# Summing the weights of a small product on VectorE instead of in the DMA, and moving stores from GpSimd's queue to ScalarE's, in a two-layer encoder trunk

## The chip, the cores and the metric

The kernel runs on one core of one Trainium2 chip. TensorE (PE in the profile) multiplies, and its weight loads are shown apart (PEld); VectorE (DVE), ScalarE (ACT) and GpSimd (POOL) work beside it, and 16 DMA engines move data. DMAs are issued by SP, by ACT or by POOL. The metric is the device time of one execution in microseconds (us); lower is better.

## The reference

The input is one sequence of 512 tokens of width 2048, all in float32. Layer 1 is gated grouped-query attention (16 heads, 4 groups of keys and values), layer 2 a gated bidirectional retention with 8 heads. After each layer comes a residual and a layer norm:

```python
proj = h @ w_in                       # layer 2: w_in is 2048 x 12288
q, k, v, g = split(proj)              # 8 heads: 256 + 256 + 512 + 512 columns a head
q, k = rope(q), rope(k) * dk ** -0.5
o = sum over both directions of (q k^T * decay) v
y = (head_group_norm(o) * silu(g)) @ w_out
x = layer_norm(ALPHA * x + y)
```

Nearly all of the arithmetic is in the projections, that is in products of a 512 x 2048 matrix with weight matrices.

## The kernel before, in words

**Products.** Each projection is computed in blocks of 1024 weight columns as two by two quarters by a scheme of the Strassen kind: seven products in place of eight, numbered 1 to 7, each of one sum of feature quarters with one sum of weight quarters. The feature sums ("forms") are made once, the weight sums are made while the weights stream in. The unit of work is a *chunk*, a 128 x 1024 piece of one product's weights in float32. ScalarE rounds it to a high part (`whi`), VectorE subtracts that from the chunk for a low part (`wlo`), both at line 122, and TensorE does three matmuls for each pair of pieces (lines 307 to 309). A chunk of a block is 12 matmuls.

**Small products.** In layer 2's input projection eight of the twelve blocks form four pairs (`PAIRED`). The two product 2s of a pair are put together and split once more into seven small products, the blocks `r_inside`; a chunk of one of them is 6 matmuls and each has two chunks. Their weights are pieces of the two blocks of the pair. A small block knows its first block as `twin`; no other block has one. The table `WITHIN` says after which chunk of the pair each chunk of a small product stands. Small product 5 needs the sum of two pieces, one from each block of the pair (quarters 11 and 12 of the small block).

**How a weight sum is made.** Some sums are made in the DMA: `onto` issues from POOL a DMA that adds its data to a tile that is already loaded. Others are made by a VectorE addition in `make`. In the kernel before, the sum of small product 5 is of the first kind: a hook at product 7 of the pair's second block calls `fetch_sum`, which loads quarter 11 by SP and then lets POOL add quarter 12. The sums of small product 3 and of the large product 6 are additions on VectorE.

**Order.** The list `order` holds all chunks in the order in which TensorE uses them. `next_chunk` keeps two chunks ready ahead of use (`AHEAD`) and, before it makes one, has fetched those up to three further on (`FETCH`). TensorE's instructions stand in the order in which the program is written. Those of the other engines are ordered by a scheduler when the program is built, with buffers as they become free in its own reckoning; at run time each engine takes its own list strictly in order, and an instruction that waits holds up all behind it. Raw pieces go to a pool of nine buffers of 128 x 1024, high and low parts to pools of three each.

**Stores.** The results of the input projection go to device memory and come back head by head: values (`vD2`), gates after SiLU (`gD2`, shown as gDr) and the rotated and transposed queries and keys (`qkD`). All of these stores are issued by POOL in the kernel before. POOL's queue also carries the adding DMAs (line 153) and the stores of the scaled residual (`yD2`). Queries and keys are copied out of TensorE's transposes by ScalarE (line 1196) right before their store, and gates come out of ScalarE's SiLU (line 1189).

**The residual.** Hooks load the first layer's output piece by piece (`load_residual`, line 1154), VectorE scales it (lines 1161 and 1162) and POOL stores it.

Of the kernel before, what the change touches and what calls it, by code (L numbers as in the profile page):

```python
# [33 lines left out]
FETCH = 3  # L34
# [15 lines left out]
PAIRED = ((2, 3), (4, 5), (6, 7), (8, 9))  # L50
# [8 lines left out]
def encoder_trunk_kernel(  # L59
# [19 lines left out]
    nc = tc.nc  # L79
# [13 lines left out]
    def nm(s):  # L93
        n_names[0] += 1
        return f"{s}{n_names[0]}"
# [4 lines left out]
    def x4(name, dt=F32R):  # L100
        return xp.tile([P, 1024], dt, tag="x", name=nm(name))

    def temp(name):
        return tmp.tile([P, 512], F32, tag="temp", name=nm(name))
# [4 lines left out]
    def in_dram(name, shape):  # L109
        return dram.tile(shape, F32, name=name)  # L110

    def v4(x):
        return x.rearrange("p (n d) -> p n d", d=P)
# [4 lines left out]
    def tcols(t):  # L118
        return slice(t * P, t * P + P)
# [10 lines left out]
    order = []  # L130

    def raw_load(src, large=False):
        raw = x4("raw", F32) if large else rp.tile([P, CH], F32, tag="raw", name=nm("raw"))
        x = nc.sync.dma_start(out=raw, in_=src)
        if fetched[0] < 12:
            in_turn(x)
        return raw

    def in_turn(x):

        tc.keep_in_program_order(x)
# [5 lines left out]
    def behind(x, y):  # L147

        tc.add_manual_dep(x.ins, y.ins.name, mybir.DependencyInfo(
            mybir.DependencyClass.NoSync, mybir.DependencyReason.DATA), reason="behind")  # L150
# [4 lines left out]
    class Block:  # L155
# [20 lines left out]
        def fetch(self, p, c):  # L176
            q = lambda n: self.quarter(n, c)
            g = self.got
            if p in (1, 2) and self.twin:
                at = 2, c + 2 * (p == 2)  # L180
                if at not in self.twin.got:
                    self.twin.got[at] = raw_load(q(11 if p == 1 else 21))
                g[p, c] = self.twin.got[at]
            elif p == 1:
                g[1 if self.first else "v", c] = raw_load(q(11), self.hold)
            elif p == 2:
                g[2, c] = raw_load(q(21))
            elif p == (3 if self.idle else 6):
                g[3, c] = raw_load(q(22), self.wide)
            elif p == 4 and self.again and not self.lean and (not self.shared or (2, c) not in g):  # L190
                g[2, c] = raw_load(q(21))
            elif p == 5 and self.first:
                if self.hold:
                    g["v", c] = g[1, c]
                else:
                    self.fetch_sum(c)
# [6 lines left out]
        def make(self, p, c):  # L203

            g, v = self.got, self.got.get(("v", c))
            if p == (3 if self.rows == 1 else 6) and (self.rows == 1 or not self.idle):
                nc.vector.tensor_add(v, v, g[3, c])  # L207
            elif p == 4 and not self.lean:
                x = nc.vector.tensor_add(v, v, g[2, c])  # L209
                if self.nc == 4:  # L210
                    behind(x, los[-3])
            if p in (3, 7):
                return g[3, c]
            return g[p, c] if p == 2 or p == 1 and self.first else v
# [53 lines left out]
    ready = []  # L268
    fetched, taken = [0], [0]

    def fetch_to(n):
        while fetched[0] < min(len(order), n):
            blk, p, c = order[fetched[0]]
            blk.fetch(p, c)
            fetched[0] += 1

    def make_chunk():
        blk, p, c = order[len(ready)]
        raw = blk.make(p, c)
        if p >= blk.keep if isinstance(blk, Plain) else p in blk.kept:  # L280
            hi, lo = x4("wkh"), x4("wkl")
        else:
            hi, lo = [wp.tile([P, CH], F32R, tag=n, name=nm(n)) for n in ("whi", "wlo")]
        los.append(split(hi, lo, raw, len(ready) < 7))
        his.append(casts[-1])
        blk.follow(p, c)
        if p == 1 and blk is a_in[1]:
            a_in[0].add_held(c, hi)
        if p == 7 and blk in r_in and blk.lean and blk.again and c in (0, 2):
            blk.add_behind(hi, blk.got["v", 2 + c // 2], 21, 2 + c // 2)  # L290
        ready.append([(half(hi, j), half(lo, j)) for j in range(2)])

    def next_chunk():

        i = taken[0]
        taken[0] += 1
        while len(ready) < min(len(order), i + 1 + AHEAD):
            fetch_to(len(ready) + 1 + FETCH)
            make_chunk()
        r = ready[i]  # L300
        ready[i] = None
        return r
# [125 lines left out]
    def turn_soon(gen, t, src, own):  # L428

        if not own:  # L430
            o = temp("c")
            nc.scalar.copy(o, src)
            src = o
        steps.append(gen(t, src))
# [29 lines left out]
    def hook(blk, p, c, fn, *args):  # L464
        blk.hooks.setdefault((p, c), []).append(lambda: fn(*args))
# [117 lines left out]
    def transpose4(src, b=None):  # L583
        b = b or bank("tr")
        for i in range(4):
            nc.tensor.transpose(out=b[:, tcols(i)], in_=src[:, tcols(i)], identity=ident)  # L586
        return b
# [3 lines left out]
    r_in = [Block(a["wr_in"][g], g < 2, again=g == 0 or any(g in p for p in PAIRED), lean=any(g == p[1] for p in PAIRED))  # L591
            for g in range(R_G)]
# [5 lines left out]
    r_inside = [Block(Quarters(a["wr_in"][i], a["wr_in"][j]), True, 2, idle=True, rows=1, twin=r_in[i])  # L598
                for i, j in PAIRED]
# [85 lines left out]
    def out_half(total, po, pl, op):  # L685


        def chunk(blk, *at):
            ks = next_chunk()
            for h in blk.hooks.get(at, ()):  # L690
                h()
            run_later()
            return ks
# [417 lines left out]
    qkD, vD2, gD2 = [[in_dram(f"{n}{h}", [P, 4, 512]) for h in range(R_HEADS)] for n in ("qkD", "vDr", "gDr")]  # L1111
# [59 lines left out]
    def rope_2(t, src, put):  # L1171

        m1, m2 = temp("m1"), temp("m2")
        xv, av, bv = [m.rearrange("p (i j r c) -> p i j r c", i=2, j=2, r=2) for m in (src, m1, m2)]
        cb, sb = [m[:, t].unsqueeze(1).broadcast_to([P, 2, 2, 64]) for m in (cos2, sin2)]
        for r in range(2):
            nc.vector.tensor_tensor(out=av[:, :, :, r], in0=xv[:, :, :, r], in1=cb, op=ALU.mult)
            nc.vector.tensor_tensor(out=bv[:, :, :, r], in0=xv[:, :, :, 1 - r], in1=sb, op=ALU.mult)
            yield
        for r in range(2):  # L1180
            nc.vector.tensor_tensor(out=av[:, :, :, r], in0=av[:, :, :, r], in1=bv[:, :, :, r],
                                    op=ALU.subtract if r == 0 else ALU.add)
        soon(3, put, m1)

    def deliver_2(blk, nb, t, src, own):
        pr, kind = divmod(r_in.index(blk), 3)
        if kind == 2:
            o = src if own else temp("gt")
            nc.scalar.activation(o, src, AF.Silu)
            nc.gpsimd.dma_start(out=gD2[2 * pr + nb][:, t], in_=o)  # L1190
        elif nb == 1:
            nc.gpsimd.dma_start(out=vD2[2 * pr + kind][:, t], in_=src)
        else:
            def put(m):
                o = temp("qkT")
                nc.scalar.copy(o, transpose4(m))  # L1196
                stored.add((2 * pr + kind, t))
                nc.gpsimd.dma_start(out=qkD[2 * pr + kind][:, :, tcols(t)], in_=v4(o))  # L1198

            turn_soon(lambda t, src: rope_2(t, src, put), t, src, own)  # L1200

# [154 lines left out]


    ev2, inside = spill(deliver_2), Inside(x2)
    hook(r_in[2], 6, 0, lambda: steps.append(inside.forms()))
    for n, (_, b) in enumerate(PAIRED):  # L1360
        for c in range(2):
            hook(r_in[b], 7, c, r_inside[n].fetch_sum, c)
    paused.append(True)
    for i in range(2):
        hook(r_in[0], 1, 2 * i, x2.form, 2, i)
    work = Stream(out_full(total, a_last, op_a[1]), in_stream(r_in, x2, ev2, (inside, put_together(deliver_2))))
    for r in range(2):
        for t in (2 * r, 2 * r + 1):
# [120 lines left out]
```

## Time and profile before

| What | Value |
|---|---|
| Median of 3 runs | 2089.72 us |
| Lowest and highest run | 2084.93 and 2091.35 us |
| Profiled execution, its time and its span | 2091.57 us, 2089.8 us |
| Mean granted TensorE clock in it | 0.997 |
| TensorE busy | 2066.4 us (99%) |
| VectorE, ScalarE, GpSimd busy | 1645.2, 1192.9, 478.2 us |
| DMA | 420.17 MB, mean 201 GB/s |

A row of the profile gives the source line, the engine, the operation, what it writes and reads by the program's names, and times in us; "idle before" is how long the engine had stood idle, and the arrow names what ended that. The busy time of TensorE is modelled from pipelined matmuls, so that a stall shows as idle time of some tenths of a microsecond less than the stretch between the starts of two matmuls.

### The profile page before, as it was taken

How to read it: one execution, taken by the hardware profiler on the slowest of the kernel's cores; microseconds unless marked ns; L12 is line 12 of the kernel's file. 1: busy time of each engine (PE TensorE's matmuls, PEld its weight loads, DVE VectorE, ACT ScalarE, POOL GpSimd, SP SyncE). 2: the span in 40 equal slices, each digit the busy share in tenths (PEclk: the TensorE clock that was granted, in tenths of full speed). 3: DMA queues.
4: the chain of work that ended last, by engine and by line, in shares of the span. 5: the costliest groups of instructions: out<-in, count | busy, mean ns of one | idle time of the engine just before them, and what ended most of it. 6: DMA issues, size and time to landing. Idle time of an engine off the chain costs nothing.

```text
span 2089.8 us, 26695 instructions
## 1 busy us (share of the span) xinstructions
PE 2066.4 (99%) x9586; PEld 1710.3 (82%) x9586; DVE 1645.2 (79%) x2224; ACT 1192.9 (57%) x1586; POOL 478.2 (23%) x579
## 2 busy tenths in 40 slices
PE   9999999999999999999999999999999999999997
PEld 7888888888888888888887788888788888888886
DVE  7788877889678887776785786876786887979786
ACT  6556546667656754554554454554456665656554
POOL 1145212122222113112213112213211122212112
PEclk9999999999999999999999999999999999999999
DMA  9777958457599879479779779879785677777875
GB/s 345 191 176 214 302 146 197 131 166 159 132 253 229 264 173 231 111 205 221 184 216 240 194 213 224 212 208 233 198 254 161 187 184 191 180 191 183 210 218 114
DMA packets 129749, 420.17 MB, mean 201 GB/s; under 512 B 15696, under 2 KB 18768, under 8 KB 129360
## 3 DMA queue, kind: packets, MB, share of 16 engines
q0 software_dynamic: 60256, 196.11, 45.8%
q1 hardware_dynamic: 68784, 221.30, 30.3%
q8 instruction: 75, 1.23, 0.2%
q10 hardware_dynamic: 576, 1.05, 0.1%
q14 instruction: 58, 0.48, 0.1%
HBM read 349.20 MB, written 71.30 MB: 201 GB/s over the span
## 4 chain that ended last, share of the span: by engine, by line
PE 86%; DMA 7%; issue 3%; DVE 2%; POOL 1%; ACT 1%; SPq 0%; POOLq 0%; ACTq 0%; DVEq 0%
PE acc L308 24%; PE acc L309 24%; PE acc L307 24%; DMA raw<-in_wr_in_dram 4%; PE tr L586 3%; PE o L307 2%; PE o L309 2%; PE o L308 2%; DMA raw<-in_wa_in_dram 1%; PE s L307 1%; PE s L309 1%; PE s L308 1%; DVE wlo L122 1%; DMA xf<-in_xq_dram 1%; ACT whi L122 1%
## 5 line engine op out<-in xcount | busy, mean ns | idle before, releaser
L122 DVE TENSOR_TENSOR wlo<-raw,whi 128x1024 fp32r<-128x1024 f32 (+1 forms) x658 | 798.9, 1219 | 317.7 <-ACT whi L122 315.0
L122 ACT CAST whi<-raw 128x1024 fp32r<-128x1024 f32 (+1 forms) x658 | 687.2, 1050 | 627.0 <-PE acc L309 456.0
L307 PE MATMUL acc<-whi,f 128*128 128x512 f32 x2464 | 972.5, 395 | 4.3 <-DVE t L646 2.4
L308 PE MATMUL acc<-wlo,f 128*128 128x512 f32 x2464 | 962.8, 391 | 5.8 <-DVE wlo L122 5.8
L309 PE MATMUL acc<-whi,f 128*128 128x512 f32 x2464 | 962.0, 390 | 0.0
L308 PEld LDWEIGHTS acc<-wlo,f 128*128 128x128 f32 x2464 | 464.1, 188 | 103.3 <-DVE wlo L122 11.8
L307 PEld LDWEIGHTS acc<-whi,f 128*128 128x128 f32 x2464 | 463.8, 188 | 97.8 <-issue 3.3
L309 PEld LDWEIGHTS acc<-whi,f 128*128 128x128 f32 x2464 | 463.4, 188 | 97.9
L153 POOL DMA_DIRECT2D raw<-in_wr_in_dram x140 | 123.4, 886 | 411.2 <-DVE wlo L122 338.2
L207 DVE TENSOR_TENSOR raw<-raw,raw 128x1024 f32<-128x1024 f32 x94 | 114.7, 1226 | 12.1 <-DMA raw<-in_wr_in_dram 8.8
L476 ACT COPY t<-acc 128x512 f32<-128x512 f32 x150 | 85.0, 587 | 44.4 <-PE acc L309 40.2
L122 DVE TENSOR_TENSOR f<-xf,f 128x1024 fp32r<-128x1024 f32 (+2 forms) x74 | 86.5, 1175 | 7.4 <-ACT f L122 7.4
L122 ACT CAST f<-xf 128x1024 fp32r<-128x1024 f32 (+2 forms) x74 | 74.7, 1015 | 20.1 <-DVE xf L362 5.5
L153 POOL DMA_DIRECT2D raw<-in_wa_in_dram x48 | 42.2, 879 | 154.8 <-DVE wlo L122 113.7
L153 POOL DMA_DIRECT2D yD<-t x48 | 43.8, 1018 | 119.9 <-DVE t L488 37.2
L569 POOL TENSOR_TENSOR rstd<-rs_e,neg_half 128x1 f32<-128x1 f32 x40 | 31.9, 797 | 171.1 <-DVE rs_e L568 170.0
L209 DVE TENSOR_TENSOR raw<-raw,raw 128x1024 f32<-128x1024 f32 x52 | 63.1, 1217 | 0.2 <-DMA raw<-in_wr_in_dram 0.2
L1198 POOL DMA_DIRECT2D qkD<-qkT x32 | 24.3, 759 | 154.4 <-ACT qkT L1196 153.8
L997 ACT ACTIVATE p<-s,nmax 128x512 f32<-128x512 f32 x64 | 44.1, 688 | 20.0 <-DVE s L995 15.1
L1279 ACT ACTIVATE o<-o,nmr,rstd 128x512 f32<-128x512 f32 x32 | 24.9, 778 | 52.4 <-DVE nmr L580 52.2
L995 DVE TENSOR_SCALAR_CACHE_REDUCE s<-s,q_rs 128x512 f32<-128x512 f32 x64 | 48.0, 752 | 7.2 <-PE s L309 6.8
L307 PE MATMUL o<-inh,pTh 128*128 128x512 f32 x128 | 51.4, 402 | 0.0
(210 smaller groups left out, 2191.6 us busy)
## 6 DMA issues: line engine op xcount, KB each, us to landing
raw<-in_wr_in_dram SPq DMA_DIRECT2D x156, 512.0 KB, 5.4
raw<-in_wr_in_dram POOLq DMA_DIRECT2D x140, 512.0 KB, 7.2
raw<-in_wa_in_dram SPq DMA_DIRECT2D x66, 512.0 KB, 6.6
raw<-in_wa_in_dram POOLq DMA_DIRECT2D x48, 512.0 KB, 7.4
raw<-in_wr_p_dram SPq DMA_DIRECT2D x36, 512.0 KB, 4.9
yD<-t POOLq DMA_DIRECT2D x48, 256.0 KB, 6.4
raw<-in_wr_p_dram POOLq DMA_DIRECT2D x24, 512.0 KB, 7.6
y<-yD SPq DMA_DIRECT2D x16, 512.0 KB, 7.2
```

What stands on the lines that cost most here:

```text
L122: x, y = nc.scalar.copy(hi, src), nc.vector.tensor_sub(lo, src, hi.bitcast(F32))
L153: return nc.gpsimd.dma_start(out=x, in_=src, accum_op=ALU.add)
L207: nc.vector.tensor_add(v, v, g[3, c])
L209: x = nc.vector.tensor_add(v, v, g[2, c])
L307: nc.tensor.matmul(ps, sh, mh, start=start, stop=False, skip_group_check=go_on)
L308: nc.tensor.matmul(ps, sh, ml, start=False, stop=False, skip_group_check=go_on)
L309: nc.tensor.matmul(ps, sl, mh, start=False, stop=stop, skip_group_check=go_on)
L476: nc.scalar.copy(keep[p, t], bk[CHAIN[p]][t])
L569: nc.gpsimd.tensor_tensor(out=dst, in0=e[:, :n], in1=neg_half[:, :n], op=ALU.pow)
L586: nc.tensor.transpose(out=b[:, tcols(i)], in_=src[:, tcols(i)], identity=ident)
L995: nc.vector.tensor_scalar(sb, sb, rs, None, op0=ALU.mult, op1=ALU.min, accum_out=nmax)
L997: nc.scalar.activation(pt, sb, AF.Exp, scale=-1.0, bias=nmax, accum_out=self.sm[t][:, h:h + 1])
```

## The change

Three edits:

- A small block now fetches both pieces for its product 5 with plain loads by SP, and `make` adds them on VectorE. The hooks that called `fetch_sum` for the small blocks are gone.
- `next_chunk` fetches further ahead by as many chunks of small products as stand among those next to be fetched.
- The stores of gates and of queries and keys in layer 2 are issued by ScalarE's queue and no longer by POOL's. The stores of values stay with POOL.

```diff
@@ fetch
+            elif p == 5 and self.twin:
+                g["v", c], g[5, c] = raw_load(q(11)), raw_load(q(12))
             elif p == 5 and self.first:
@@ make
+            elif p == 5 and self.twin:
+                nc.vector.tensor_add(v, v, g.pop((5, c)))
             elif p == 4 and not self.lean:
@@ next_chunk
         while len(ready) < min(len(order), i + 1 + AHEAD):
-            fetch_to(len(ready) + 1 + FETCH)
+            n = len(ready) + 1 + FETCH
+            fetch_to(n + sum(b in r_inside for b, _, _ in order[len(ready):n]))
             make_chunk()
@@ deliver_2
             nc.scalar.activation(o, src, AF.Silu)
-            nc.gpsimd.dma_start(out=gD2[2 * pr + nb][:, t], in_=o)
+            nc.scalar.dma_start(out=gD2[2 * pr + nb][:, t], in_=o)
...
                 stored.add((2 * pr + kind, t))
-                nc.gpsimd.dma_start(out=qkD[2 * pr + kind][:, :, tcols(t)], in_=v4(o))
+                nc.scalar.dma_start(out=qkD[2 * pr + kind][:, :, tcols(t)], in_=v4(o))
@@ hooks of layer 2
-    for n, (_, b) in enumerate(PAIRED):
-        for c in range(2):
-            hook(r_in[b], 7, c, r_inside[n].fetch_sum, c)
```

What it moves is seen in the built programs' instruction lists. TensorE's is the same. First VectorE, in the first pair, shortly ahead of the place where small product 5 is used; line 479 before is line 484 after, `wlo` is the low part of a chunk, `raw` a loaded piece. Before:

```order
L479 TENSOR_TENSOR t_8592<-acc_8443,t_8592 128x512
L122 TENSOR_TENSOR wlo_8670<-raw_8462,whi_8669 128x1024
L122 TENSOR_TENSOR wlo_8692<-raw_8480,whi_8691 128x1024
L122 TENSOR_TENSOR wlo_8711<-raw_8647,whi_8710 128x1024
L122 TENSOR_TENSOR wlo_8728<-raw_8251,whi_8727 128x1024
L484 TENSOR_TENSOR t_8518<-t_8518,acc_8344 128x512
```

After:

```order
L484 TENSOR_TENSOR t_8592<-acc_8443,t_8592 128x512
L122 TENSOR_TENSOR wlo_8670<-raw_8462,whi_8669 128x1024
L211 TENSOR_TENSOR raw_8704<-raw_8704,raw_8706 128x1024
L122 TENSOR_TENSOR wlo_8689<-raw_8480,whi_8688 128x1024
L122 TENSOR_TENSOR wlo_8709<-raw_8647,whi_8708 128x1024
L211 TENSOR_TENSOR raw_8725<-raw_8725,raw_8727 128x1024
L122 TENSOR_TENSOR wlo_8730<-raw_8240,whi_8729 128x1024
L489 TENSOR_TENSOR t_8518<-t_8518,acc_8344 128x512
```

The two additions (line 211) now stand between the low parts of chunks that come well before small product 5; the low part of small product 5's own first chunk stands some rows further on. The other three pairs read alike.

Then POOL's queue in the second pair, where line 153 are the adding DMAs and line 1190 the stores of gates. Before:

```order
L153 DMA raw_9849<-in_wr_in_dram 128x1024
L1190 DMA gDr_5785<-t_9702 128x512
L1190 DMA gDr_5785<-t_9704 128x512
L153 DMA raw_9990<-in_wr_in_dram 128x1024
L1190 DMA gDr_5784<-gt_10071 128x512
L153 DMA raw_10009<-in_wr_in_dram 128x1024
L1190 DMA gDr_5784<-gt_10074 128x512
L153 DMA raw_10021<-in_wr_in_dram 128x1024
L153 DMA raw_10039<-in_wr_in_dram 128x1024
```

After:

```order
L153 DMA raw_9853<-in_wr_in_dram 128x1024
L153 DMA raw_9964<-in_wr_in_dram 128x1024
L153 DMA raw_9982<-in_wr_in_dram 128x1024
L153 DMA raw_10001<-in_wr_in_dram 128x1024
L153 DMA raw_10020<-in_wr_in_dram 128x1024
```

The adding DMAs now follow each other without stores between them. Last ScalarE in the fourth pair, with the copy of a transposed query or key (line 1196 before, 1201 after). Before:

```order
L122 CAST whi_12731<-raw_12587 128x1024
L1196 COPY qkT_12740<-tr_12741 128x512
L122 CAST whi_12760<-raw_12600 128x1024
L476 COPY t_12777<-acc_12296 128x512
L476 COPY t_12779<-acc_12297 128x512
```

After:

```order
L122 CAST whi_12747<-raw_12571 128x1024
L1201 COPY qkT_12756<-tr_12757 128x512
L1203 DMA qkD_5772<-qkT_12756 512x1x128
L122 CAST whi_12776<-raw_12583 128x1024
L481 COPY t_12793<-acc_12310 128x512
L481 COPY t_12795<-acc_12311 128x512
```

The store stands right behind its copy and ahead of the next high part. On SP two loads are added in each pair (four stand where two stood), and one load of gates changes places with its neighbour later on.

## The prediction

> **What bounds the kernel now.** I read the page's busy times first, then TensorE's waits, then the single stalls in the timeline, then the chain of waits behind each.
>
> ```profile
> PE 2066.4 (99%) x9586; PEld 1710.3 (82%) x9586; DVE 1645.2 (79%) x2224; ACT 1192.9 (57%) x1586; POOL 478.2 (23%) x579
> PE acc L308 <- DVE wlo L122: 6.5, 10, 1.9
> PE acc L307 <- DVE t L646: 2.4, 1, 2.4
> PE acc L307 <- ACT whi L122: 2.1, 2, 1.8
> ```
>
> TensorE is the bound, and the change leaves its list as it was. So it can win only what TensorE loses in stalls, and lose what it adds to them. Waits of TensorE sum to some 11 us; those in layer 2's input projection, where all edits lie, are these:
>
> ```profile
> 983.79 0.50 PE L308 MATMUL acc<-wlo,f 128*128 128x512 f32 x1 [0.70 <-DVE wlo L122]
> 1136.23 0.50 PE L307 MATMUL acc<-whi,s 128*128 128x512 f32 x1 [0.37 <-ACT whi L122]
> 1137.49 0.50 PE L308 MATMUL acc<-wlo,s 128*128 128x512 f32 x1 [0.76 <-DVE wlo L122]
> 1139.88 0.50 PE L308 MATMUL acc<-wlo,f 128*128 128x512 f32 x1 [0.77 <-DVE wlo L122]
> 1169.58 0.47 PE L307 MATMUL acc<-whi,f 128*128 128x512 f32 x1 [2.42 <-DVE t L646]
> 1296.74 0.50 PE L308 MATMUL acc<-wlo,f 128*128 128x512 f32 x1 [0.69 <-DVE wlo L122]
> 1449.46 0.50 PE L308 MATMUL acc<-wlo,f 128*128 128x512 f32 x1 [0.34 <-DVE wlo L122]
> 1478.97 0.47 PE L307 MATMUL acc<-whi,f 128*128 128x512 f32 x1 [1.77 <-ACT whi L122]
> 1507.36 0.50 PE L308 MATMUL acc<-wlo,f 128*128 128x512 f32 x1 [1.95 <-DVE wlo L122]
> ```
>
> Two of them cost more than their length:
>
> ```profile
> 1170.80:1174.20 3.40, 3.40 (x9) 2.64 (x8) 3.40 (x4) 1.28 (x2) 0.22 (x1) 0.50 0.57 186
> 1508.70:1512.10 3.40, 3.40 (x10) 2.66 (x9) 2.77 (x4) 0.75 (x1) 0.93 (x2) 0.50 0.89 149
> ```
>
> These are stretches of the table of windows; the third number from the end is TensorE's granted clock. After the idle 2.42 and 1.95 us the clock is halved for 3.4 us, which costs 1.7 us each time; after 1.77 it is not. [...]
>
> **Part 1, the removed sum in the DMA.** In each of the four pairs stalls of the list above end such a chain (first pair, the low part and the matmul of 983.79 follow):
>
> ```profile
> 958.01 7.08 DMA raw<-in_wr_in_dram
> 965.71 13.22 DMA raw<-in_wr_in_dram
> 979.03 1.06 ACT whi L122
> ```
>
> The load takes 7.1 us, the adding DMA behind it 13.2, and small product 5's second chunk is cast when it lands. These six stalls (at 983.79, 1136 to 1140, 1296.74, 1449.46) are 0.70 + 0.37 + 0.76 + 0.77 + 0.69 + 0.34 = 3.6 us idle. A matmul after a stall also shows 0.50 us in place of 0.39 and the next starts late, some 0.25 us a stall by my estimate, together **-5.1**. Both pieces will be plain loads, so nothing waits for 13 us any more.
>
> **Part 2, the first addition waits.** VectorE takes its list in order, and the additions stand early in it. In the trace:
>
> ```profile
> 959.48 1.23 DVE L122 TENSOR_TENSOR wlo<-raw,whi 128x1024 fp32r<-128x1024 f32 x1 [0.30 <-ACT whi L122]
> 962.24 1.23 DVE L122 TENSOR_TENSOR wlo<-raw,whi 128x1024 fp32r<-128x1024 f32 x1 [1.53 <-ACT whi L122]
> 964.92 1.22 DVE L122 TENSOR_TENSOR wlo<-raw,whi 128x1024 fp32r<-128x1024 f32 x1 [1.45 <-ACT whi L122]
> 967.68 1.22 DVE L122 TENSOR_TENSOR wlo<-raw,whi 128x1024 fp32r<-128x1024 f32 x1 [1.54 <-ACT whi L122]
> 958.19 0.39 PE L307 MATMUL acc<-whi,f 128*128 128x512 f32 x1
> 958.42 0.39 PE L308 MATMUL acc<-wlo,f 128*128 128x512 f32 x1
> ```
>
> The first addition comes behind the low part of 959.48, which ends at 960.7. Its second piece takes the place of the load issued at 958.01 (the buffers come free in the same order), and that landed at 965.1: VectorE stands still for over 4 us, with the low part of 962.24 behind it. How much may that be late? A high part starts when TensorE has left the chunk three before (three buffers); two chunks of 12 matmuls at 0.227 us, 5.44, are then ahead of its first use, and cast and low part take 2.3: a slack of 3.1. The low part that ended at 963.47 must be there by 966.6. It would end at 965.1 + 1.23 + 1.14 = 967.5: a stall of 0.9. In general this stall is the load's time less 6.2. The same load in the other pairs:
>
> ```profile
> 1112.39 8.68 DMA raw<-in_wr_in_dram
> 1270.99 7.15 DMA raw<-in_wr_in_dram
> 1424.07 6.96 DMA raw<-in_wr_in_dram
> ```
>
> That gives 2.5, 1.0 and 0.8, together **+5.2**, which I take: the adding DMA that falls away is posted when these loads are nearly over (965.71). Bounds: 0 if they take the median of 5.4 (table of DMA issues, below), 5.2 as they stand. The pair with 2.5 would stand idle longer than the 1.95 that halved the clock: **+1.7**.
>
> **Part 3, the second addition waits.** It stands behind the low part of 964.92. Its second piece can use only the buffer that the first addition frees (so it is in the build), so its load is issued at about 965.1 + 1.26 = 966.4. The low part behind it, due at 972.0 (967.68 + 1.22 + 3.1) plus the 0.9 already lost, ends 2.4 after this load lands. The stall is T - 4.1, with T the load's time.
>
> ```profile
> raw<-in_wr_in_dram SPq DMA_DIRECT2D x156, 512.0 KB, 5.4
> raw<-in_wr_in_dram SPq DMA_DIRECT2D x6, 512.0 KB, 7.7
> 956.00:983.00 27.00, 27.00 (x120) 22.05 (x118) 16.27 (x16) 11.27 (x12) 6.05 (x10) 1.00 1.02 283
> q0 software_dynamic: 60256, 196.11, 45.8%
> q1 hardware_dynamic: 68784, 221.30, 30.3%
> ```
>
> The median over the program is 5.4, in this stretch (956 to 983) 7.7, with the DMA engines full (share 1.02). By the queues' rows, 196.11 MB cost 45.8% of the span by POOL and 221.30 MB 30.3% by SP, so half a megabyte costs 2.6 us of all engines by POOL and 1.5 by SP. Two adding DMAs become two loads: 2.1 us less work in a full stretch of 27. With that and only one load ahead in SP's queue I take 5.4: 1.25 a pair, **+5.0**; bounds 0 and, at 7.7, 14.4. The additions themselves, 8 x 1.23 = 10 us, lie in VectorE's idle time (16.3 us busy of those 27) and would cost that much if it had none.
>
> **Part 4, stores leave POOL's queue.** Behind the stall of 1169.58 is an addition on VectorE that waited for a load:
>
> ```profile
> 1166.47 1.23 DVE L207 TENSOR_TENSOR raw<-raw,raw 128x1024 f32<-128x1024 f32 x1 [3.76 <-DMA raw<-in_wr_in_dram]
> 1158.17 8.21 DMA raw<-in_wr_in_dram
> 1142.94 0.56 POOL L1190 DMA_DIRECT2D gDr<-gt  x1 [0.56 <-ACT gt L1189]
> ```
>
> The load was slow beside POOL's backlog, in which this store and the next token half's stood. Each is 256 KB, 1.3 us at POOL's rate; without them the backlog ends 2.6 us sooner, out of a wait of 3.76. I take the stall down from 2.7 to 0.7, which spares the half clock too: **-3.7**, bounds 0 and -4.4. The stall of 1507.36 ends this chain:
>
> ```profile
> 1492.47 0.54 POOL yD L1163
> 1493.14 4.07 DMA qkD<-qkT
> 1497.26 8.13 DMA res<-nD
> 1491.66 0.58 ACT L1196 COPY qkT<-tr 128x512 f32<-128x512 f32 x1
> ```
>
> The load of the residual waits for a buffer that the store of a key empties; the store waits in POOL's queue behind another. The copy is done at 1492.24, so ScalarE can issue 0.9 sooner, and its issue is shorter than POOL's. I take 1.2 us off a stall of 2.2, again with the half clock: **-2.9**, bounds 0 and -3.9. The stall of 1478.97 waits for an adding DMA that stays: 0.
>
> **Part 5, ScalarE issues 64 stores.**
>
> ```profile
> L792 ACTq DMA_DIRECT2D xf<-in_xq_dram x4: 393/430/454, 0.7 to 2.2; - x4
> ```
>
> At 0.43 us each that is 27.5 us of ScalarE, queued ahead of high parts. The slack of 3.1 us of a chunk covers one store: 0; if a quarter were uncovered, +7. Fetching further ahead is in Parts 2 and 3: loads go out as buffers come free, not as the list would like.
>
> **Sum.** -5.1 + 5.2 + 1.7 + 5.0 - 3.7 - 2.9 = +0.2 us on the profiled 2091.57, that is 2091.8. That execution lay 1.85 above the median of 2089.72, so the forecast is 2089.9 us: a wait is moved from the DMA's sum to VectorE's additions, and the rest nearly cancels.
>
> **Rivals.**
>
> - *The additions don't wait.* With less work on the DMA engines the loads take 4 to 5.4 us, Parts 2 and 3 are 0: -5.1 - 3.7 - 2.9 = -11.7, 2078.0. For it: the engines are the full resource there, and they get 2.1 us less. Against: the load of Part 2 is over before the removed work begins.
> - *VectorE is held longer (slower).* If the second load takes the stretch's 7.7 us, each pair idles 3.6 us at line 122's second low part, and each time the clock halves: -5.1 + 5.2 + 14.4 + 4 x 1.7 - 6.6 = +14.7, 2104.4. It decides from T of about 6.3, where the idle passes 1.95 us. For it: the crowded stretch; against: the 2.1 us again.
> - *The stores bring nothing,* since what is moved is the queue and not the bytes: -5.1 + 5.2 + 1.7 + 5.0 = +6.8, 2096.5. For it: the engines are shared by all queues and full. Against: the key's store did wait 0.9 us for POOL alone. [...]
> - *ScalarE's stores delay high parts:* +7, 2097.
>
> **How the numbers follow.** About 0.3% (6.3 us) is what a measurement can tell from no change here. Chances: forecast 0.55, additions that don't wait 0.22, VectorE held 0.08, stores without effect 0.13, ScalarE 0.02. The forecast's own range is 2084 to 2095. The bounds of Parts 2 to 4 reach both ways, so the range is 2078 to 2098, which leaves out half of the first rival and nearly all of the second. Faster: 0.19 of the first rival and 0.04 of the forecast, 0.23. Slower: 0.08, half of 0.13, 0.02 and little else, 0.16. No change: 0.61.
>
> **What would show it.** In the profile after, a row of VectorE's waits "raw L211 from DMA raw" of 20 us or more over 8 times, and TensorE waiting for `wlo` some 15 us ahead of where it now does, would bear out Parts 2 and 3; no such row would be the first rival. TensorE's idle time near 1169.6 and 1507.4 below 1 us, and a granted clock of 1.00 behind both, would bear out Part 4. A load of residual that still starts 5 us after the copy, or high parts that wait behind stores on ScalarE, would make it wrong.

## The result, and the profile after

The changed kernel takes 2101.15 us (median of 6 runs, 2095.61 to 2104.34), the kernel before 2088.72 (6 runs, 2084.93 to 2091.35). The ratio is 1.0057, with a 95% interval of 1.0040 to 1.0074: slower by 0.6%, some 12 us, where 2089.9 was forecast. (A ratio is estimated from all runs of both kernels and can differ by up to 0.1% from the quotient of the medians. The kernel before was measured anew beside each group of experiments, so kernels of different groups are compared by their ratios.) The profiled execution took 2100.0 us, 8.4 more than that of the kernel before.

The table of waits of the kernel after (engine, line, what was waited for, total us, times, longest), TensorE first, then VectorE:

```profile
PE acc L313 <- DVE wlo L122: 11.9, 7, 4.2
PE acc L312 <- DVE t L651: 5.1, 3, 3.0
DVE raw L211 <- DMA raw<-in_wr_in_dram: 32.1, 8, 7.8
DVE raw L209 <- DMA raw<-in_wr_in_dram: 9.1, 4, 4.4
```

The new row is the third: VectorE stands still 32 us at the eight new additions (line 211), for their loads. TensorE's wait for low parts rose from 6.5 to 11.9. Where, the rows of TensorE with an idle time in the timeline of the kernel after tell:

```profile
966.58 0.50 PE L313 MATMUL acc<-wlo,f 128*128 128x512 f32 x1 [1.98 <-DVE wlo L122]
1126.32 0.79 PE L313 MATMUL acc<-wlo,f 128*128 128x512 f32 x1 [4.18 <-DVE wlo L122]
1175.17 0.47 PE L312 MATMUL acc<-whi,f 128*128 128x512 f32 x1 [3.01 <-DVE t L651]
1288.45 0.50 PE L313 MATMUL acc<-wlo,f 128*128 128x512 f32 x1 [1.82 <-DVE wlo L122]
1294.29 0.47 PE L312 MATMUL acc<-whi,f 128*128 128x512 f32 x1 [0.33 <-DVE t L489]
1443.52 0.50 PE L313 MATMUL acc<-wlo,f 128*128 128x512 f32 x1 [2.08 <-DVE wlo L122]
1450.14 0.47 PE L312 MATMUL acc<-whi,f 128*128 128x512 f32 x1 [1.08 <-ACT whi L122]
1490.63 0.47 PE L312 MATMUL acc<-whi,f 128*128 128x512 f32 x1 [1.65 <-DVE t L651]
```

The six short stalls of the pairs before (3.6 us together) are gone. In their place each pair has one of about 2 us, the second one of 4.2, some 15 us ahead of the old place. Three of the stalls have a half clock behind them, as the table of windows of the kernel after shows (third number from the end):

```profile
967.50:970.50 3.00, 3.00 (x9) 2.32 (x8) 1.19 (x2) 0.00 (x0) 0.90 (x1) 0.50 0.91 315
1126.00:1131.00 5.00, 4.68 (x11) 3.72 (x12) 3.37 (x4) 0.00 (x0) 0.86 (x1) 0.50 0.92 254
1175.80:1178.60 2.80, 2.80 (x8) 2.20 (x7) 2.65 (x3) 1.86 (x2) 0.00 (x0) 0.50 0.67 258
1441.00:1447.00 6.00, 3.92 (x17) 2.89 (x17) 3.50 (x3) 1.66 (x2) 0.88 (x1) 1.00 0.99 286
```

In the first pair VectorE's timeline of the kernel after shows what holds it:

```profile
957.35 1.23 DVE L122 TENSOR_TENSOR wlo<-raw,whi 128x1024 fp32r<-128x1024 f32 x1 [0.30 <-ACT whi L122]
964.17 1.23 DVE L211 TENSOR_TENSOR raw<-raw,raw 128x1024 f32<-128x1024 f32 x1 [5.59 <-DMA raw<-in_wr_in_dram]
965.31 2.35 DVE L122 TENSOR_TENSOR wlo<-raw,whi 128x1024 fp32r<-128x1024 f32 x2
969.47 1.23 DVE L211 TENSOR_TENSOR raw<-raw,raw 128x1024 f32<-128x1024 f32 x1 [1.81 <-DMA raw<-in_wr_in_dram]
```

The addition of 964.17 waits 5.6 us, and the low part behind it (965.31) is the one that TensorE waits for at 966.58.

For all profiles the table below gives, for the stretches in question, what TensorE lost there: the time from the start of the stretch's first matmul to the start of the first one behind it, less 0.227 us for each matmul and some 0.11 for each transpose, the time between their starts where nothing waits (958 to 964 and 413.4 in the kernel before). A stretch holds the same matmuls in every kernel. "Pairs" are the four stretches that in the kernel before lie at 956 to 986, 1113 to 1148, 1272 to 1301 and 1430 to 1456, the last three columns those around the old stalls of 1169, 1479 and 1507 (1148 to 1179, 1456 to 1486, 1486 to 1521). Half clocks are in it. Each row is one execution, whose own time is given.

| Kernel (line of the experiment below) | Profiled, us | Pairs | 1169 | 1479 | 1507 |
|---|---|---|---|---|---|
| before | 2091.57 | 5.2 | 4.3 | 2.2 | 4.1 |
| before, second profile | 2089.28 | 4.5 | 3.7 | 2.4 | 2.0 |
| after | 2100.00 | 16.9 | 4.9 | 2.1 | 0.2 |
| after, second profile | 2099.01 | 15.4 | 4.5 | 2.2 | 0.2 |
| sum and further fetch | 2101.15 | 14.8 | 4.4 | 3.9 | 2.0 |
| sum alone | 2096.45 | 13.8 | 3.9 | 2.2 | 0.2 |
| stores alone | 2084.04 | 3.1 | 4.2 | 2.3 | 0.2 |
| additions late | 2094.68 | 6.9 | 4.6 | 4.2 | 0.2 |
| additions late, stores by GpSimd | 2087.53 | 6.6 | 2.3 | 2.2 | 1.1 |
| additions later by two | 2084.98 | 2.4 | 4.5 | 2.3 | 0.7 |
| values later | 2096.99 | 12.0 | 4.5 | 2.2 | 0.2 |
| all additions later | 2083.89 | 2.8 | 0.0 | 0.2 | 5.1 |
| before, with product 6's additions later | 2087.83 | 5.5 | 0.0 | 0.2 | 2.6 |
| all additions and the residual later | 2079.36 | 2.5 | 0.0 | 0.2 | 0.2 |

The pairs went from 5.2 to 16.9, 11.7 us, nearly all of the 12 between the medians. The 1507 column went from 4.1 to 0.2, which in the two profiled executions hides a part of it. Outside the columns the kernel after loses 1.3 us more near 1209, where VectorE waits 4.5 us for a load of the residual, and 0.9 near 1660.

### The profile page after: what moved, and what is told of

It is laid out like the page before. It is cut to its first block, busy times and chain, and to the rows that moved or that the text cites. A ratio compares the mean times of both kernels' runs of the same rounds, so it can differ in the third digit from the quotient of the medians.

```text
span 2098.2 us, 26653 instructions
## 1 busy us (share of the span) xinstructions
PE 2066.6 (98%) x9586; PEld 1711.7 (82%) x9586; DVE 1653.6 (79%) x2232; ACT 1195.0 (57%) x1586; POOL 431.7 (21%) x507
## 3 DMA queue, kind: packets, MB, share of 16 engines
q1 hardware_dynamic: 69936, 225.50, 30.9%
## 4 chain that ended last, share of the span: by engine, by line
PE 92%; DMA 4%; DVE 2%; issue 1%; ACT 1%; SPq 0%; DVEq 0%; POOLq 0%; POOL 0%; ACTq 0%
PE acc L313 26%; PE acc L314 26%; PE acc L312 26%; PE tr L591 3%; DMA raw<-in_wr_in_dram 3%; PE o L312 2%; PE o L314 2%; PE o L313 2%; PE s L312 1%; PE s L314 1%; PE s L313 1%; DVE wlo L122 1%; ACT whi L122 1%; DMA res<-nD 0%; PE tr L1137 0%
## 5 line engine op out<-in xcount | busy, mean ns | idle before, releaser
L313 PE MATMUL acc<-wlo,f 128*128 128x512 f32 x2464 | 963.1, 391 | 11.9 <-DVE wlo L122 11.9
L153 POOL DMA_DIRECT2D raw<-in_wr_in_dram x132 | 115.0, 871 | 622.0 <-DVE wlo L122 525.7
L122 DVE TENSOR_TENSOR pTl<-tr,pTh 128x512 fp32r<-128x512 f32 x64 | 43.6, 684 | 8.9 <-ACT pTh L122 8.7
```

Source lines behind the costliest of these rows:

```text
L122: x, y = nc.scalar.copy(hi, src), nc.vector.tensor_sub(lo, src, hi.bitcast(F32))
L153: return nc.gpsimd.dma_start(out=x, in_=src, accum_op=ALU.add)
L313: nc.tensor.matmul(ps, sh, ml, start=False, stop=False, skip_group_check=go_on)
```

## The experiments

**The parts of the change apart.** Two ways of explaining the loss: theory A, the additions hold VectorE up; theory B, the stores on ScalarE's queue cost the time. First the sum and the further fetch, with the stores as before:

```diff
-            nc.scalar.dma_start(out=gD2[2 * pr + nb][:, t], in_=o)
+            nc.gpsimd.dma_start(out=gD2[2 * pr + nb][:, t], in_=o)
...
-                nc.scalar.dma_start(out=qkD[2 * pr + kind][:, :, tcols(t)], in_=v4(o))
+                nc.gpsimd.dma_start(out=qkD[2 * pr + kind][:, :, tcols(t)], in_=v4(o))
```

> The sum on VectorE and the further fetch alone; all stores stay with GpSimd. Theory A (the additions hold VectorE up; the stores are worth a few us at most): in the profile after, the four pairs cost 0.8 + 4.3 + 2.0 + 3.0 = 10 us against before, so this kernel is 8 to 13 us slower than before (2097 to 2102), with VectorE waiting some 30 us at the addition of line 211, and the stall near 1507 is still there. Theory B (the stores on ScalarE's queue cost the time, the sum is about neutral): within 4 us of before, 2085 to 2093.

Measured: 2094.76 us against 2086.20 of the kernel before, ratio 1.0047 (1.0033 to 1.0060). That is 8.6 us slower by the medians, inside the 8 to 13 us of theory A, though below the 2097 that it named.

Then the stores alone: the two lines of the change at `gD2` and `qkD`, and nothing else of it.

> The stores on ScalarE's queue alone; sum in the DMA and fetch distance as before. Theory A: 0 to 4 us faster than before (2085 to 2089): the stall near 1507 with its half clock is gone (4 us), the one near 1169 stays at 2 to 3 us idle. Theory B: 5 to 12 us slower (2094 to 2101), with new stalls outside the pairs.

Measured: 2086.86 against 2086.20, ratio 1.0004 (0.9994 to 1.0014). The stores neither cost nor bring anything that can be measured. Theory B falls, and so does the prediction's gain of 6.6 us from them; by the interval they bring 1.3 us at most. TensorE's row of the stall that Part 4 was to shorten, in the timeline of the kernel with the stores alone:

```profile
1166.41 0.47 PE L307 MATMUL acc<-whi,f 128*128 128x512 f32 x1 [2.35 <-DVE t L646]
```

2.42 before, 2.35 now: taking the gates out of GpSimd's queue did not shorten it. The other stall of Part 4, that of 1507, is not there in this profile. VectorE's wait for its load of the residual, before and with the stores alone:

```profile
1505.48 0.69 DVE L1161 SCALAR_TENSOR_TENSOR res<-res,ln_gain 128x512 f32<-128x512 f32 x1 [4.74 <-DMA res<-nD]
```

```profile
1497.01 0.69 DVE L1161 SCALAR_TENSOR_TENSOR res<-res,ln_gain 128x512 f32<-128x512 f32 x1 [0.60 <-DMA res<-nD]
```

Last the sum alone, without the further fetch:

```diff
-            n = len(ready) + 1 + FETCH
-            fetch_to(n + sum(b in r_inside for b, _, _ in order[len(ready):n]))
+            fetch_to(len(ready) + 1 + FETCH)
```

(against the kernel with sum and further fetch.)

> The sum on VectorE alone: fetch distance and stores as before. If the further fetch is of no account, 2092 to 2098, as with sum and further fetch (2094.8), with the wait at line 211 near 30 us. If the further fetch is what crowds the buffers, 2085 to 2089. If the further fetch helps the loads, above 2100 with a longer wait at line 211.

Measured: 2096.74 against 2086.59, ratio 1.0057 (1.0039 to 1.0075). VectorE's row in its table of waits:

```profile
DVE raw L211 <- DMA raw<-in_wr_in_dram: 31.0, 8, 7.1
```

The sum alone does all of it; the further fetch is of no account that these runs could tell (1.0047 with it, 1.0057 without).

**How steady the single stalls are.** Both kernels once more, unchanged, for a second profile.

> The kernel before, unchanged, for a second profile. Its profiled execution of 2091.57 is at the top of its own runs (2082 to 2091, median 2086.2). If its stalls are the same every time, TensorE again stands idle 2 us and more near 1169.6 and 1507.4, each with a half clock behind it. If they come and go, one or both are missing, and the terms of the prediction that took 6.6 us from them rested on one execution.

> The changed kernel, unchanged, for a second profile. Theory A (additions hold VectorE) says that the wait at line 211 is again near 32 us over 8 times and that the four first stalls of the pairs are there again with 2 to 4 us each; the stalls elsewhere (1175, 1209, 1490) may differ.

Measured: before 2089.28, after 2099.01. The pairs come out alike both times (5.2 and 4.5; 16.9 and 15.4), and the wait at line 211 was 30.9 us. The stall of 1507 does not: 4.1 in the first profile of before, 2.0 in the second, 0.2 with the sum alone, where GpSimd still issues every store. So its size changes without the stores having moved. It goes with them all the same: VectorE's wait for that load is 3.4 to 4.9 us in five of the six profiles with all stores by GpSimd, and at most 0.6 in six of the seven with stores by ScalarE in which the residual's place is unchanged (5.8 in all additions later).

**The place of the additions.** `behind(x, y)` tells the scheduler to put x later than y in its engine's list. First each addition not ahead of the low part of the chunk just before its own, which puts it four low parts later:

```diff
-                nc.vector.tensor_add(v, v, g.pop((5, c)))
+                behind(nc.vector.tensor_add(v, v, g.pop((5, c))), los[-1])
```

> The whole change, but each addition on VectorE may not be placed ahead of the low part of the chunk just before its own (it stands 4 to 5 low parts later in VectorE's list); loads, buffers and additions are the same in number. Theory A: VectorE's wait at the addition falls from 32 us to under 5, the first stalls of the pairs are gone, and with the old stalls of the pairs gone too (5 us) and the stores' 2 to 4 us the time is 2080 to 2086, faster than before. Theory B: the place of the additions is not the cause, 2096 or more. Rival C (the wait only moves: the load of the second piece is late for the low part of small product 5 itself): 2088 to 2096, with TensorE waiting for that low part at the chunk of small product 5.

Measured: 2091.94 against 2086.20, ratio 1.0033 (1.0020 to 1.0046). The wait at line 211 is gone, and the pairs fell from 16.9 to 6.9, as theory A has it. But the time did not come below before: rival C's range. The next addition waits instead; VectorE's row in the table of waits of this kernel, then of the kernel before (where the line is 207):

```profile
DVE raw L209 <- DMA raw<-in_wr_in_dram: 18.4, 9, 4.1
```

```profile
DVE raw L207 <- DMA raw<-in_wr_in_dram: 8.8, 5, 3.8
```

Four of its nine waits, 1.7 to 2.0 us each, are new and lie in the pairs. The likely reason, which no run tests, is that an addition that stands late holds its two buffers longer, so that the loads of small product 3 go out later and that product's addition waits for them.

The same with the stores by GpSimd again:

> As the kernel with the late additions, but all stores by GpSimd as before, so the sum by itself without the wait. Theory A: the old stalls of the pairs are gone, 5 us faster than before: 2081 to 2086; the difference from the kernel with the late additions and ScalarE's stores is what the stores are worth, 0 to 4 us. Theory B: this kernel is 5 us or more faster than the late one with the stores on ScalarE.

Measured: 2092.86, ratio 1.0031 (1.0017 to 1.0045); the wait at line 209 is 16.1 us. None of the theories had this: 5 us faster than before was expected, 6 slower was found. Again the stores make no difference (2091.94 and 2092.86). In the profiles of the two late kernels the pairs lose some 1.5 us more than before, not 6. In the first, another 2.0 us lie in the 1479 column and 2.7 between 1320 and 1380, where an addition of line 209 and a scaling of the residual (4.7 us) wait for their loads. The second shows neither, but its profiled execution was its fastest by far (2087.53): where the rest of its 6 us lies stays open.

So a place between: two low parts later than in the change, two earlier than in the late ones.

```diff
-                behind(nc.vector.tensor_add(v, v, g.pop((5, c))), los[-1])
+                behind(nc.vector.tensor_add(v, v, g.pop((5, c))), los[-3])
```

> The whole change, with each addition not ahead of the low part three chunks before its own: two low parts later than in the changed kernel, two earlier than in the late one, whose additions kept their buffers long and made the next addition (line 209, small product 3) wait 18 us in place of 9. Theory A: VectorE waits 1 to 2 us at each first addition, inside TensorE's slack of 3.1 us, the wait at line 209 is back near 9 us, and the time is 2080 to 2087, not slower than before. Rival D (it is the work of the additions and their loads in this stretch, wherever they stand): 2090 to 2095, as with the late ones.

Measured: 2084.66 against 2086.59, ratio 1.0000 (0.9988 to 1.0011). VectorE's table of waits:

```profile
DVE raw L209 <- DMA raw<-in_wr_in_dram: 13.9, 7, 4.0
DVE raw L211 <- DMA raw<-in_wr_in_dram: 6.2, 5, 2.4
```

The waits at line 211 fell from 32 to 6 us, each short enough for TensorE's slack (2.4 at the longest, of the 3.1 us that the prediction worked out), and the pairs lose 2.4 us. Loads, additions, fetch distance and stores are those of the changed kernel; 0.57% hung on two places in VectorE's list. Rival D is out. The wait at line 209 did not fall to 9 as expected, only to 13.9; in three of the pairs it is still some 2 us.

**Why the loads were slower than taken.** The chain of waits of the kernel after has these loads of the second piece, one a pair:

```profile
955.88 8.16 DMA raw<-in_wr_in_dram
1113.40 10.38 DMA raw<-in_wr_in_dram
1277.90 8.05 DMA raw<-in_wr_in_dram
1432.71 8.27 DMA raw<-in_wr_in_dram
```

7.08, 8.68, 7.15 and 6.96 were taken from before. GpSimd's timeline has, in the kernel after and then in the kernel before, the two stores of values that small product 5's stretch begins with:

```profile
956.82 1.13 POOL L1197 DMA_DIRECT2D vDr<-t  x2 [2.83 <-DVE t L484]
```

```profile
962.47 1.40 POOL L1192 DMA_DIRECT2D vDr<-t  x2
```

Before, they stood in GpSimd's queue behind small product 5's adding DMA, which had to wait for its load (it went out at 961.9). With that DMA gone they go out 5.6 us earlier, 0.9 us after the start of the load of the second piece, where it was 4.5. To test this, the two stores were tied to a later chunk by a one-column copy on GpSimd that reads its high part:

```diff
+            def put_v():
+                if t < 2:
+                    in_turn(nc.gpsimd.tensor_copy(small("nmax"), ready[-1][0][0][:, 0:1].bitcast(F32)))
+                x = nc.gpsimd.dma_start(out=vD2[2 * pr + kind][:, t], in_=src)
+                if t < 2:
+                    in_turn(x)
+            if t < 2:
+                soon(3, put_v)
+            else:
+                put_v()
-            nc.gpsimd.dma_start(out=vD2[2 * pr + kind][:, t], in_=src)
```

> The changed kernel, with the two stores of values that GpSimd issues beside the load of the second piece (at 956.8 and 957.4 in the profile after; at 962.5 and 963.2 in the kernel before, where they stood behind an adding DMA that waited for its load) made to wait for the high part three chunks later. The load of the second piece took 8.16, 10.38, 8.05 and 8.27 us in the changed kernel. If these early stores are what lengthened it over the 7 us of before, it falls to 7.0 to 7.4 in pairs 0, 2 and 3 (in pair 1 gates, not values, are stored there, so it stays), the stalls there fall from 2 to about 1 us, without half clocks, and the time is 2094 to 2098. If the load is slow for other reasons, it stays at 8 us and the time at 2099 to 2102.

Measured: 2095.50 against 2087.48, ratio 1.0039 (1.0025 to 1.0053). Its chain of waits and one of the stores in GpSimd's timeline:

```profile
957.71 6.85 DMA raw<-in_wr_in_dram
1113.13 10.50 DMA raw<-in_wr_in_dram
1275.27 7.01 DMA raw<-in_wr_in_dram
1431.76 6.78 DMA raw<-in_wr_in_dram
```

```profile
969.20 0.89 POOL L1200 DMA_DIRECT2D vDr<-t  x1
```

The loads took 6.85, 7.01 and 6.78 in the three pairs with values and 10.50 in the one without, as the theory said. The stores went out at 969.2, later still than before, and the pairs' loss fell from 16.9 to 12.0. The time lies in that theory's range too, though the interval of its ratio overlaps with the changed kernel's (1.0040 to 1.0074).

**The same fault elsewhere.** The stall near 1169 that Part 4 put down to GpSimd's backlog looks like this on VectorE in the kernel after:

```profile
1172.07 1.23 DVE L209 TENSOR_TENSOR raw<-raw,raw 128x1024 f32<-128x1024 f32 x1 [4.36 <-DMA raw<-in_wr_in_dram]
1173.21 1.22 DVE L122 TENSOR_TENSOR wlo<-raw,whi 128x1024 fp32r<-128x1024 f32 x1
1174.35 0.68 DVE L651 TENSOR_TENSOR t<-t,acc 128x512 f32<-128x512 f32 x1
```

TensorE waits for the subtraction of line 651, which frees an accumulator, and that stands behind an addition (line 209, large product 6) that waits for its load. With these additions held back as well:

```diff
-                nc.vector.tensor_add(v, v, g[3, c])
+                x = nc.vector.tensor_add(v, v, g[3, c])
+                if self in r_in:
+                    behind(x, los[-3])
```

> A version that may beat both: the additions of small product 5 later by two low parts as in the run before this one, and the additions of the large product 6 in layer 2 also not ahead of the low part three chunks before their own, so that the subtraction into t (line 651) that frees an accumulator stands ahead of an addition that waits for its load. If the stalls near 1166 and 1475 (2.6 and 1.8 us idle, with a half clock behind the first) come from that addition as the trace says, they are gone: 4 to 6 us off 2084.7, that is 2078 to 2081. If TensorE needs the load's chunk just as late, the wait moves to a low part and the time is 2083 to 2087.

Measured: 2083.89 against 2087.48, ratio 0.9982 (0.9973 to 0.9991). The columns 1169 and 1479 go to 0.0 and 0.2. The time fell less than the 4 to 6 us expected, since a stall near 1496 took part of it back (5.1 in the last column).

The kernel before with that edit alone:

> The kernel before with only the additions of the large product 6 in layer 2 not ahead of the low part three chunks before their own; sum in the DMA, fetch distance and stores as before. If the stalls near 1169 and 1478 come from the place of that addition, 3 to 6 us faster than before, 2081 to 2084; if not, as before, 2085 to 2088. Its distance to the version with all additions later is what the change itself is worth once no addition waits: some 3 us (the old stalls of the pairs, 3.6 us idle).

Measured: 2085.63 against 2087.48, ratio 0.9993 (0.9984 to 1.0003). The two stalls are gone here too, with all stores by GpSimd, which settles what they came from. The time, though, is within what can be told from before; 3 to 6 us were expected. In the profile a new stall, 3.2 us idle up to 1355.12 with a half clock behind it (in the chain a matmul takes 0.43 us at 1355.91, and 0.23 ahead of the stall), takes back 5 of the 6 us gained; VectorE waits there 7.1 us for a load of the residual. What the change itself is worth once no addition waits is the distance of these two, 0.9982 and 0.9993, whose intervals overlap: 2 us, not told from nothing.

In the version with all additions later the stall near 1496 is VectorE's wait for the residual. From its table of waits, its chain and VectorE's timeline:

```profile
DVE res L1168 <- DMA res<-nD: 11.0, 3, 5.8
1487.99 9.26 DMA res<-nD
1497.33 0.69 DVE L1168 SCALAR_TENSOR_TENSOR res<-res,ln_gain 128x512 f32<-128x512 f32 x1 [5.81 <-DMA res<-nD]
1497.94 1.22 DVE L122 TENSOR_TENSOR wlo<-raw,whi 128x1024 fp32r<-128x1024 f32 x1
```

Once more an instruction that waits for a load, ahead of a low part. It too was held back:

```diff
-        nc.vector.scalar_tensor_tensor(out=f, in0=f, scalar=ALPHA, in1=res["ln_gain"], op0=ALU.mult, op1=ALU.mult)
+        behind(nc.vector.scalar_tensor_tensor(out=f, in0=f, scalar=ALPHA, in1=res["ln_gain"], op0=ALU.mult, op1=ALU.mult), los[-1])
```

> The version with all additions later, and the scaling of the residual also not ahead of the low part just written before it in the program. In that version one stall of 3.0 us idle is left near 1495: VectorE waits 5.8 us for a load of the residual, which took 9.3 us, with a low part behind it. If that is the same mechanism once more, the stall is gone, 3 to 5 us off 2083.9: 2079 to 2081. If the residual's buffers, held longer, delay the results that need them, the time is 2084 to 2090.

Measured: 2078.88 us (2077.89 to 2080.39) against 2085.11, ratio 0.9970 (0.9959 to 0.9981). This version beats both kernels. Its table of waits has for TensorE:

```profile
PE acc L315 <- DVE wlo L122: 3.1, 6, 0.7
```

That 0.7 us is the longest idle time of TensorE in layer 2's projection now, and VectorE's table has no row for the residual any more.

## Why the prediction was wrong

**What bounds the kernel: right.** TensorE's work was the same (9586 matmuls in both, 2066.4 us busy before and 2066.6 after), and nearly the whole difference lies in its stalls and the half clocks behind them.

**Part 1, -5.1: right.** The six stalls that waited for the adding DMA are gone from the pairs. As a gain of the kernel the term is too large, though: with the additions held back the pairs still lose 2.4 to 2.8 us, against 3.1 to 5.5 in the four profiles with the sum in the DMA.

**Part 2, the first addition waits: the mechanism right, the size off.** The stall was to be the load's time less 6.2. With the times measured that is 1.96, 4.18, 1.85 and 2.07 us; idle were 1.98, 4.18, 1.82 and 2.08. But the term was worked out with the load times of before (7.08, 8.68, 7.15, 6.96), on the ground that the removed work lies behind these loads. It overlooked that GpSimd's queue, once the DMA that waited in it was gone, lets the stores behind that DMA go out earlier, into the same stretch. That this is the cause the run with the values later shows for three pairs. In the second pair gates are stored there and not values, and what took its load from 8.68 to 10.38 us is not settled. The traces point to the same cause: two stores of gates go out 2.0 us after that load starts, 5.0 before; with sum and further fetch alone, where GpSimd issues them, TensorE's longest wait for a low part is 3.4 us in place of 4.2. No run tests it. In all, 5.2 us of idle time became 10.1.

The half clock was taken once, 1.7 us. It came twice in the pairs, by the trace from 967.32 to 970.73 and from 1124.33 to 1131.16, of which 4.8 us lie behind the stall. Matmuls start 0.43 us apart there (967.43, 967.86, 968.28) in place of 0.23, so that of the 3.4 and 4.8 us some 1.6 and 2.3 are lost.

**Part 3, the second addition waits, +5.0: too large.** The first addition ended at 965.40 and the second started at 969.47, so its load took no more than 4.1 us where 5.4 was taken, and the low part behind it was in time. What is left near the second additions are idle times of 0.33 and 1.08 us in two pairs.

**Part 4, the stores, -6.6: wrong.** This is the step that failed outright. Alone, the stores made the ratio 1.0004. The stall of 1169 (-3.7) hung on the place of an addition in VectorE's list, not on GpSimd's backlog: it stayed at 2.35 us with the stores alone and is gone, with all stores by GpSimd, once that addition is held back. So is the stall of 1478.97, which the prediction put down to an adding DMA. For the stall of 1507 (-2.9) the chain was read rightly, and the sign that it set, idle time below 1 us there, came. But its size was one execution's: in the second profile of before it is 1.40 us, and the 2.0 us lost there in all leave no room for a half clock (1.6 us). And every profile with stores by ScalarE has new idle time of 0.4 to 0.9 us behind the projection, where TensorE waits for VectorE's `o` (0.75 at 1659.75 in the kernel after), which no profile with all stores by GpSimd has. The rival that the stores bring nothing was right on this (1.0004).

**Part 5, ScalarE issues 64 stores, 0: right** by the same run.

With these sizes, and nothing for Part 4, the sum is -5.1 + 10.1 + 4 x 0.25 (the late start behind a stall) + 3.9 (half clocks) + 1.4 = +11.3 us, against 11.7 that the pairs lost in the profile and 12.4 between the medians.

**The rivals.** "VectorE is held longer" had the side and, at 2104.4, nearly the time, but it put the wait at the second addition; it was the first. "The stores bring nothing" was true as far as it went, and at 2096.5 lacked the longer loads. The forecast set against a cost whose mechanism it had right, and whose size it had too small, a gain (Part 4) that was read from two stalls of a single execution, one of them with the wrong cause.

## What to carry to other kernels

Before an instruction that waits for a load is put on an engine that works its list in order, look at what stands behind it: here TensorE paid what of its wait the next low part had no slack for (5.6 us of wait, 2.0 of stall in the first pair), and a `behind` of two places took away what the whole change had cost (1.0057, then 1.0000). Held back too far, the next addition waited in its place (1.0033), so the place has two sides. When a waiting DMA leaves a queue, ask what was held up behind it: here those transfers went out 5.6 us earlier, next to the load that was needed most, which took 8.16 us where it had taken 7.08. And a gain read from one stall of one execution wants a second profile first.

## What was not expected of the hardware

The granted clock did not go by the length of the idle time alone. It was halved after TensorE stood idle 1.95 us (at 1507.36 before) and 1.98 (at 966.58 after), and not after 2.08 (at 1443.52 after, where the window from 1441 to 1447 has a clock of 1.00) nor 1.82 (at 1288.45 after, 1.00 from 1286 to 1292). What went with it in the first profiles of the two kernels is how the idle time lay in a grid of equal time steps. In the kernel after the granted clock changed at 967.32, 970.73, 1124.33, 1131.16, 1175.53 and 1178.95, in the kernel before at 1170.78, 1174.19, 1508.70 and 1512.11, the start and the end of the execution apart. From one change to the next these are 1, 45, 2, 13 and 1 times 3.4133 us in the one and 1, 98 and 1 times in the other, to within 0.01 us. Windows cut along this grid, for the stalls of 1.98 and 2.08 us in the kernel after (behind the comma stands TensorE's busy time, third from the end its clock):

```profile
963.91:967.32 3.41, 1.44 (x7) 0.89 (x6) 3.15 (x3) 1.04 (x1) 0.00 (x0) 1.00 1.06 259
967.32:970.73 3.41, 3.41 (x9) 2.64 (x9) 1.60 (x3) 0.00 (x0) 0.90 (x1) 0.50 0.91 310
1438.36:1441.77 3.41, 3.08 (x14) 2.23 (x12) 0.67 (x1) 1.53 (x2) 0.00 (x0) 1.00 1.03 378
1441.77:1445.19 3.42, 1.67 (x7) 1.39 (x8) 2.83 (x3) 0.57 (x1) 0.23 (x1) 1.00 1.04 283
1445.19:1448.60 3.41, 3.41 (x16) 2.80 (x16) 1.56 (x2) 1.06 (x1) 0.65 (x1) 1.00 0.92 262
```

The 1.98 us lie inside one step; the 2.08 are split into 0.33 and 1.75. With all steps of the two profiles cut so, the start and the end apart, six are followed by a step at half clock: they had 1.95, 1.98, 1.98, 2.20, 2.21 and 3.01 us idle, one of those with 1.98 at half clock itself (from 1124.33 after). Of the others none had more than 1.75 (from 1441.77 after). Six steps of two executions show no more than that. From the start of the span the first change lies 343.0 steps off in the kernel before and 283.4 in the kernel after, so the grid did not lie alike in the two, and whether a given stall fell into one step or into two was luck. Of the three stalls of some 2 us in the pairs one halved the clock in the first profile of the kernel after. Its second profile lost 1.5 us less in the pairs (15.4 and 16.9), which would fit one half clock fewer at 1.6 us; that is an estimate.
